# Stick-breaking logits that stay in their PSUM banks, decay products over 128 rows, and the scheduler's price of a matmul column

## The chip, the cores and the metric

The kernel runs on one core of a Trainium2 chip. The metric is the device time of one execution in microseconds (us), taken as the median of the runs; lower is better. Five engines are named as the profile names them: PE (TensorE, its weight loads apart as PEld), DVE (VectorE), ACT (ScalarE), POOL (GpSimd) and SP (SyncE, which issues most DMAs).

## What is computed

The reference is a network of two blocks on 512 tokens of width 1024, all in float32: a short convolution mixer, a gated feed-forward layer, a sparse attention layer ("NSA") and another feed-forward layer; then the second block, which has two mixers side by side, a state-space mixer ("SSD") and a stick-breaking attention of 16 heads, and a third feed-forward layer. The change touches the stick-breaking attention and one product of the SSD mixer:

```python
def stick_breaking_mixer(q, k, v, q_norm_w, k_norm_w):
    ...
        logits = jnp.einsum("bhqd,bhkd->bhqk", qb, kp) * scale
        strict = s_pos[None, :] < t_pos[:, None]
        log_rem = jnp.where(strict, jax.nn.log_sigmoid(-logits), 0.0)
        log_between = lax.cumsum(log_rem, axis=3, reverse=True) - log_rem
        weights = jnp.where(strict, jnp.exp(jax.nn.log_sigmoid(logits) + log_between), 0.0)
        outs.append(jnp.einsum("bhqk,bhkd->bhqd", weights, vp))

def ssd_chunked(x, dt, a, b_mat, c_mat):
    ...
    a_cs = jnp.cumsum(a_dt, axis=-1)
    seg = a_cs[..., :, None] - a_cs[..., None, :]
    decay = jnp.exp(jnp.where(causal, seg, -jnp.inf))
```

For a key s before a query t, the log of the weight is the logit minus the sum of softplus(logit) over the keys from s up to the query.

## The kernel before

**Products.** A float32 product is made of three: each operand is split into a rounded part and a rest (`hilo`, names ending in h and l), and PE multiplies h by h, l by h and h by l, 512 columns at most at a time, into one PSUM bank of 128 x 512. There are eight banks (tag `ps`), and every PSUM tile takes one whole bank from its first product to its last reader. Weights come from HBM in chunks (`raw`), are split by ACT and DVE (`wh`, `wl`) and multiply with the tokens (tiles `d`, and `qk` for the token-major queries, keys and values).

**Stick-breaking.** Each of the 16 heads goes through two generators. `sb_logits` handles the four key tiles of 128 keys in three units: 384 and 128 columns in the first, 256 in the second, 512 in the third. For each unit it multiplies the keys `ks` with the queries `qh` and `ql` into a bank `lg`, and makes the softplus from it: three ACT passes (Abs, Exp, Ln), a DVE pass (`le<-lg,le`), a POOL mask (AFFINE_SELECT), and the split into `ph` and `pl`, which are kept in SBUF. The bank `lg` is free after the DVE pass. `sb_out` comes later: for each unit it takes a new bank `bt`, makes the same logits in it once more (`bt<-qh,ks` and `bt<-ql,ks`), adds the sums of the softplus terms onto them with constant matrices (`ntri`, `nones`, and the mask `rmask` by an identity; all of them are slices of the tile `cr`), and ACT takes the exponential (`we`). The split of that (`w`) is multiplied with the values into `so`. The places in the code:

```python
            todo = [(k, st["qh"][h][:, 128 * kt:512], 0), (k, st["ql"][h][:, 128 * kt:512], 0)]
            todo += [(self.ntri, x[:, o:o + n], 0) for x in ps[u]]
            todo.append((self.ridn, self.rmask, None))
```

**Decay products.** In `ssd_pair`, `weights(h)` spreads one row of the running sums over all partitions with a product `al<-at,er`: the tile `at` has 64 rows (the rounded sums in rows 0 to 15, the rests in rows 32 to 47, zeros between) and `er` picks one of them. There is one such product of 512 columns per head, 16 in all.

**The order.** Nothing runs in the order in which it is written. A `Recorder` notes every instruction; `arrange` then orders them for each engine by a model of its own: `cost` gives each a duration, `forward` lets each engine take what is ready, `backward` gives latest starts, which serve as priorities in the next `forward`. It also chooses the PSUM bank of each tile and, where several engines can do an instruction (`any`), the engine. All helpers issue through one line, so the profile shows L485 for nearly everything: go by tile names. In `weave`, the generators of the second block stand side by side: for each pair of heads the projections, `ssd_pair`, `sb_logits`, `sb_out`, with start and end set by constants (`P0` to `P13`, `SS`, `O0` to `O3`).

Of the kernel before, what the change touches and what calls it, by code (L numbers as in the profile page):

```python
# [11 lines left out]
D = 1024  # L12
# [74 lines left out]
def weave(*streams):  # L87
    """emits instruction streams side by side: (generator, the total of what it yields, start, end)"""
# [21 lines left out]
class View:  # L110
    """an access pattern of a tile that gets its place when the instructions are ordered"""
# [21 lines left out]
class Slot:  # L133
    """one tile as the program sees it, from its first access to its last"""
# [21 lines left out]
class Recorder:  # L156
    """records the instructions of the program, orders those of every engine by the time at which their
    operands are there and by their place in the program, and gives the tiles their places"""
# [8 lines left out]
    # from the end on one engine to the start on another  # L167
# [27 lines left out]
    def any(self, *ways):  # L195
        """one instruction that several engines can do, the usual one first: (engine, method, arguments)"""
# [45 lines left out]
    def cost(self, o, method, a, k, outs, ins):  # L242
        """nanoseconds on the engine, and those of a transfer"""
# [3 lines left out]
        # a scalar per partition  # L247
# [4 lines left out]
        elif o.eng == "tensor":  # L252
            passes = 1 if ins[-1].dtype == F32R else 2 if method == "transpose" else 6
            o.dur = size(outs[0]) * passes / 2.4 + 3.0
            # the next product waits until its own matrix is loaded
            o.load = (int(ins[0].ap.shape[-1]) if method == "matmul" else 128) / 1.2
# [13 lines left out]
    def place(self, ap):  # L270
        """the pattern on the place its tile got"""
# [23 lines left out]
    def backward(self):  # L295
        """the latest starts, from the end of the program"""
# [30 lines left out]
    def forward(self, urgent, look, timed=False):  # L327
# [26 lines left out]
        def avail(t):  # L354
            """when the tile can have a place, or None"""
# [15 lines left out]
        def begin(e, i, limit):  # L371
            """when the engine can start the instruction, or None if not by the limit"""
# [14 lines left out]
            if e in other:  # L387
                # one engine at a time reads a bank
                for t in o.banks:
                    at = max(at, t.read.get(other[e], -1e9) + self.LAG[other[e]][e])  # L390
            if e != o.eng:
                # another engine has to be done with it earlier than the usual one
# [8 lines left out]
        while first < len(ops):  # L401
            best = None
            for e, lst in cand.items():
# [10 lines left out]
                if top is not None and timed and e in self.PATIENT:  # L414
                    # a more urgent one that is ready soon goes first if that makes the later of the two less late
# [74 lines left out]
class Body:  # L490
# [26 lines left out]
    def alike(*views):  # L517
        """whether the Pool engine can do it: in SBUF, on the same partitions, of a size that is worth it"""
# [22 lines left out]
    def copy(self, out, a, scale=None):  # L541
        """a, by a factor"""
# [21 lines left out]
    def load(self, g, parts=None):  # L564
        """starts the transfer of a group of weight blocks"""
# [59 lines left out]
    def dense_g(self, name, n, x, ks=None, m=128):  # L625
        """the same as dense, in steps"""
# [7 lines left out]
    def dense_seq(self, specs, x, ks=None, first=2, late=1):  # L634
        """yields the finished PSUM tile of every (name, n); the late operands are used last in the first tiles,
        or every operand in all of them before the next one"""
# [10 lines left out]
    def dense_halves(self, specs, x, ks=None):  # L647
        """the same for the halves of the tokens, the first halves of all tiles before the second ones"""
# [12 lines left out]
    def dense_late(self, specs, x, first):  # L661
        """dense_seq where the second halves of the tokens come later: the first tiles take them last"""
        out = [self.ps("d") for _ in range(first)]
        for h, sl in enumerate(HALVES):
            for (name, n), p in zip(specs, out):
                # one accumulation group per bank: its first write clears the bank's flags
                self.half(p[:, sl], name, n, x, range(len(x)), sl, h == 0, h == 1)
# [5 lines left out]
    def rsq(self, src, scale, eps):  # L673
        """rsqrt(scale * src + eps) by logarithm and exponential, and a step of Newton"""
# [10 lines left out]
    def allsum(self, acc):  # L685
        """the sums over the partitions, on all of them"""
# [35 lines left out]
    def setup(self):  # L722
# [18 lines left out]
        self.er = self.nc.tile([64, 16], F32R, "er")  # L741
        nc.vector.tensor_copy(self.er, self.cst[0:64, C_E:C_E + 16])
# [965 lines left out]
```

## Time and profile before

| | us |
|---|---|
| median of three timed runs | 2162.2 (2161.71 to 2162.23) |
| the profiled execution, first to last instruction | 2159.8 |
| PE busy in it | 2117.5 |
| DVE busy | 1386.1 |
| ACT busy | 941.8 |
| stretch of the stick-breaking mixer, 1327 to 1759 | 432 |

The profiled execution is told by its span, from the first to the last instruction: 2159.8 us. The timed runs take 2.4 us more, which lie around the span. A row of the timeline has the start, the duration, the engine, and out<-in by tile. Ends of matmuls are modelled, and they overlap: the pace of PE is read from the starts of rows that follow each other.

### The profile page before, as it was taken

The page shows a single profiled execution, that of the slowest core. Times are in us where ns is not written, and L with a number is a line of the kernel's source. Part 1 is how long each engine was busy: PE and PEld are TensorE (multiplying, and loading weights), DVE is VectorE, ACT ScalarE, POOL GpSimd, SP SyncE. Part 2 cuts the span into 40 slices and gives each one's busy share as a digit, 9 for nine tenths or more (in the row PEclk, how much of TensorE's full clock was granted, in tenths as well). Part 3 has the DMA queues.
Part 4 walks back from the last instruction along what each step waited for, and adds up shares of the span by engine and source line. Part 5 has one row for each costly group of instructions (what it writes and reads, how often), then busy time and mean ns, then how long its engine had stood idle before and what let it go on. Part 6 is the DMA issues. An engine that isn't in the chain of part 4 may idle for free.

```text
span 2159.8 us, 28829 instructions
## 1 busy us (share of the span) xinstructions
PE 2117.5 (98%) x11113; PEld 1789.1 (83%) x11113; DVE 1386.1 (64%) x2347; ACT 941.8 (44%) x1587; POOL 425.9 (20%) x558
## 2 busy tenths in 40 slices
PE   8999999999999999999999999999999998999999
PEld 7888888888788777888888887989897888888887
DVE  6578754644868996654355598787879867333333
ACT  4233322332335885322222477677667746222221
POOL 1023320211223763000000141221315222000000
PEclk9999999999999999999999999999999999999999
DMA  4245652533332000222222332111121124222222
GB/s 166 98 178 188 212 183 97 175 117 104 104 127 72 1 1 31 97 98 98 98 98 98 117 127 79 59 50 59 59 69 40 40 95 140 98 98 98 98 98 98
DMA packets 60682, 214.04 MB, mean 99 GB/s; under 512 B 7424, under 2 KB 7552, under 8 KB 60544
## 3 DMA queue, kind: packets, MB, share of 16 engines
q1 hardware_dynamic: 52704, 186.50, 24.9%
q0 software_dynamic: 7840, 25.70, 3.5%
q8 instruction: 87, 1.43, 0.3%
q14 instruction: 51, 0.42, 0.1%
HBM read 210.07 MB, written 2.10 MB: 98 GB/s over the span
## 4 chain that ended last, share of the span: by engine, by line
PE 86%; DVE 9%; ACT 2%; issue 2%; POOL 1%; DMA 0%; SPq 0%; DVEq 0%; ACTq 0%; POOLq 0%
PE d L485 71%; PE qk L485 5%; PE bt L485 2%; PE o L485 2%; DVE wl L485 1%; PE so L485 1%; PE pt L485 1%; PE s L485 1%; DVE pr L485 1%; PE lg L485 1%; DVE e L485 1%; DVE ptl L485 1%; ACT wh L485 1%; DVE ss L485 0%; PE chid L485 0%
## 5 line engine op out<-in xcount | busy, mean ns | idle before, releaser
L485 ACT CAST wh<-raw 128x1024 fp32r<-128x1024 f32 (+1 forms) x332 | 347.6, 1048 | 873.1 <-PE d L485 736.8
L485 DVE TENSOR_TENSOR wl<-raw,wh 128x1024 fp32r<-128x1024 f32 (+1 forms) x342 | 424.6, 1242 | 417.3 <-ACT wh L485 414.5
L485 PE MATMUL d<-xh,wh 128*128 128x512 f32 (+1 forms) x1064 | 417.4, 394 | 6.0 <-ACT xh L485 6.0
L485 PE MATMUL d<-xh,wl 128*128 128x512 f32 (+1 forms) x1064 | 416.5, 392 | 1.0 <-DVE wl L485 1.0
L485 PE MATMUL d<-xl,wh 128*128 128x512 f32 x1064 | 416.3, 391 | 0.0
L485 PE MATMUL d<-hb,wh 128*128 128x512 f32 (+1 forms) x1136 | 332.7, 377 | 3.6 <-ACT hb L485 3.3
L485 PEld LDWEIGHTS d<-xh,wh 128*128 128x128 f32 (+1 forms) x1064 | 200.5, 189 | 47.6 <-ACT xh L485 6.0
L485 PEld LDWEIGHTS d<-hb,wh 128*128 128x128 f32 x1136 | 205.5, 190 | 40.1 <-ACT hb L485 3.5
L485 PEld LDWEIGHTS d<-xh,wl 128*128 128x128 f32 (+1 forms) x1064 | 200.3, 188 | 43.7 <-DVE wl L485 1.8
L485 PEld LDWEIGHTS d<-xl,wh 128*128 128x128 f32 x1064 | 200.4, 188 | 41.6 <-issue 0.7
L485 PE MATMUL d<-hb,wl 128*128 128x512 f32 (+2 forms) x568 | 212.3, 376 | 2.5 <-DVE wl L485 2.5
L485 PE MATMUL d<-hidh,wl 128*128 128x512 f32 (+1 forms) x561 | 211.8, 378 | 0.0
L485 PE MATMUL d<-hidh,wh 128*128 128x512 f32 (+1 forms) x561 | 211.5, 377 | 0.0
L485 PE MATMUL d<-hidl,wh 128*128 128x512 f32 (+1 forms) x561 | 211.5, 377 | 0.0
L485 PE MATMUL qk<-wh,hb 128*128 128x256 f32 x768 | 145.0, 288 | 2.1 <-ACT hb L485 1.0
L485 POOL TENSOR_TENSOR acc<-acc,sq 128x512 f32<-128x512 f32 (+1 forms) x24 | 38.2, 1591 | 499.7 <-ACT sq L485 441.9
L485 PEld LDWEIGHTS qk<-wh,hb 128*128 128x128 f32 x768 | 121.8, 193 | 6.5 <-DVE hb L485 1.5
L485 PEld LDWEIGHTS d<-hb,wl 128*128 128x128 f32 (+1 forms) x568 | 107.3, 190 | 22.6 <-DVE wl L485 3.5
L485 PEld LDWEIGHTS d<-hidl,wh 128*128 128x128 f32 x561 | 105.6, 188 | 19.4
L485 PEld LDWEIGHTS d<-hidh,wh 128*128 128x128 f32 x561 | 105.6, 188 | 19.3
L485 PEld LDWEIGHTS d<-hidh,wl 128*128 128x128 f32 x561 | 105.6, 188 | 19.2
L485 PE MATMUL qk<-wl,hb 128*128 128x256 f32 x384 | 109.0, 286 | 1.5 <-DVE wl L485 1.5
(370 smaller groups left out, 3678.5 us busy)
## 6 DMA issues: line engine op xcount, KB each, us to landing
raw<-in_wall_dram SPq DMA_DIRECT2D x345, 512.0 KB, 3.2
ada<-in_wada_dram POOLq DMA_DIRECT2D x96, 256.0 KB, 4.6
res<-in_x_dram SPq DMA_DIRECT2D x8, 256.0 KB, 7.3
out_dram<-res SPq DMA_DIRECT2D x8, 256.0 KB, 2.0
raw<-in_wall_dram SPq DMA_DIRECT2D x2, 256.0 KB, 3.7
cond<-in_c_dram POOLq DMA_DIRECT2D x2, 256.0 KB, 5.3
cst<-in_consts_dram SPq DMA_DIRECT2D x1, 394.5 KB, 7.0
mst<-in_consts_dram SPq DMA_DIRECT2D x1, 320.0 KB, 3.8
```

Of the source, the lines that this page charges most:

```text
L485: r = getattr(getattr(self.real, o.eng), m)(*[self.place(x) for x in a], **{n: self.place(x) for n, x in k.items()})
```

## The change

Three edits, and no other that does anything (comments and docstrings went too).

First, `sb_logits` leaves its logits in the bank `lg`, with the accumulation open, and hands the bank on with `ph` and `pl`. `sb_out` takes no bank of its own and makes no logits: it adds the sums onto that bank. So a bank is held from the first logits product of a unit to its exponential. Only the first product into the bank has the start flag.

Second, `at` and `er` have 128 rows in place of 64, the added rows zero.

Third, the scheduler's model of a matmul: a column costs 17/16 of a 2.4 GHz cycle (it was one cycle), the fixed part is 1 ns (it was 3), and a weight load is 3 ns dearer. The constants in `weave` are as before.

```diff
+    COLUMN = 17 / 16 / 2.4
...
-            o.dur = size(outs[0]) * passes / 2.4 + 3.0
-            # the next product waits until its own matrix is loaded
-            o.load = (int(ins[0].ap.shape[-1]) if method == "matmul" else 128) / 1.2
+            o.dur = size(outs[0]) * passes * self.COLUMN + 1.0
+
+            o.load = (int(ins[0].ap.shape[-1]) if method == "matmul" else 128) / 1.2 + 3.0
...
-        self.er = self.nc.tile([64, 16], F32R, "er")
-        nc.vector.tensor_copy(self.er, self.cst[0:64, C_E:C_E + 16])
+        self.er = self.nc.tile([128, 16], F32R, "er")
+        nc.vector.tensor_copy(self.er, self.cst[:, C_E:C_E + 16])
...
-        self.at = self.pg(F32R, "at")[0:64]
+        self.at = self.pg(F32R, "at")
...
-            mm(al, self.er[:, hd:hd + 1].to_broadcast([64, 128]), self.at, start=True, stop=True)
+            mm(al, self.er[:, hd:hd + 1].to_broadcast([128, 128]), self.at, start=True, stop=True)
...
+            for i, (kt, o, n) in enumerate(self.UNITS[u]):
+                k = st["k"][h][:, 128 * kt:128 * kt + 128]
+
+                for x in ("qh", "ql"):
+                    self.nc.tensor.matmul(lg[:, o:o + n], k, st[x][h][:, 128 * kt:512], start=i == 0 and x == "qh",
+                                          stop=False, skip_group_check=True)
...
-            ps.append(self.hilo(e, w, name="p"))
+            ps.append(self.hilo(e, w, name="p") + (lg,))
...
-            b = self.ps("bt")
-            # log weight: logit - (sum of the softplus terms from this key to the query)
+            b = ps[u][2]
...
-                todo = [(k, st["qh"][h][:, 128 * kt:512], 0), (k, st["ql"][h][:, 128 * kt:512], 0)]
-                todo += [(self.ntri, x[:, o:o + n], 0) for x in ps[u]]
-                todo.append((self.ridn, self.rmask, None))
+                todo += [(self.ntri, x[:, o:o + n], b[:, o:o + n]) for x in ps[u][:2]]
+                todo.append((self.ridn, self.rmask, b[:, o:o + 128]))
...
+            for j, (mat, x, dst) in enumerate(todo):
+                mm(dst, mat, x, start=False, stop=j == len(todo) - 1, skip_group_check=True)
```

PE has 11099 products before and 10971 with the change; the 128 that are missing are the second logits, 8 per head. The new prices and the missing products reorder all engines. Two places on PE are shown here, with the numbers of the tiles.

The sums of the 512-column unit of the first head, before: a bank of their own, which starts with the two logits products.

```order
L485 MATMUL bt_11715<-qh_11195,ks_11298 128x512
L485 MATMUL bt_11715<-ql_10600,ks_11298 128x512
L485 MATMUL bt_11715<-ph_11622,cr_73 128x512
L485 MATMUL bt_11715<-pl_11637,cr_73 128x512
L485 MATMUL bt_11715<-cr_73 128x128
L485 MATMUL bt_11715<-ph_11444,cr_73 128x384
L485 MATMUL bt_11715<-pl_11467,cr_73 128x384
```

The same sums with the change, in the bank that the logits were left in; the products of the SSD mixer (`y`) follow after the third.

```order
L486 MATMUL lg_11537<-ph_11597,cr_73 128x512
L486 MATMUL lg_11537<-pl_11607,cr_73 128x512
L486 MATMUL lg_11537<-cr_73 128x128
L486 MATMUL y_11649<-mh_11554,xdh_11412 64x128
L486 MATMUL y_11649<-ml_11564,xdh_11412 64x128
```

The two logits products are gone, and the rest of the sums stands further on.

The second place is in the middle of the mixer, where the first half of the output projection (`d<-ysh`, `share` in the code) starts: the 256-column logits of a head and what follows them. Before:

```order
L485 MATMUL lg_13718<-qh_13029,ks_13024 128x256
L485 MATMUL lg_13718<-ql_13048,ks_13024 128x256
L485 MATMUL d_13724<-ysh_13689,wh_13414 128x512
L485 MATMUL d_13726<-ysh_13689,wh_13641 128x512
L485 MATMUL d_13724<-ysl_13710,wh_13414 128x512
L485 MATMUL d_13724<-ysh_13689,wl_13443 128x512
L485 MATMUL d_13724<-ysh_13694,wh_13414 128x512
```

With the change, where `ph_13684` and `pl_13689` are the two parts of the softplus of these very logits:

```order
L486 MATMUL lg_13664<-qh_12963,ks_12974 128x256
L486 MATMUL lg_13664<-ql_12959,ks_12974 128x256
L486 MATMUL lg_13561<-ph_13684,cr_73 128x256
L486 MATMUL lg_13664<-ph_13684,cr_73 128x256
L486 MATMUL d_13696<-ysh_13687,wh_13358 128x512
L486 MATMUL lg_13561<-pl_13689,cr_73 128x256
L486 MATMUL lg_13561<-ph_13612,cr_73 128x128
L486 MATMUL lg_13561<-pl_13618,cr_73 128x128
```

Before, the products of the projection follow the logits; with the change the sums over these logits' own softplus stand right behind them, with no product between. At two more places of the new order few products stand between a unit's logits and the first product with its `ph`: 14 (a 256-column unit) and 16 (the 512-column unit after it). The next smallest are 23 and 33; in the order before, no unit has fewer than 50 there.

## Rows read from the trace of the kernel before

**Rows 1.** The page, its first lines: span, busy time of the engines.
```profile
span 2159.8 us, 28829 instructions
PE 2117.5 (98%) x11113; PEld 1789.1 (83%) x11113; DVE 1386.1 (64%) x2347; ACT 941.8 (44%) x1587; POOL 425.9 (20%) x558
```

**Rows 2.** Windows: start:end, length, busy by engine, granted clock, DMA share, GB/s.
```profile
567.00:842.00 275.00, 263.91 (x1614) 215.89 (x1613) 236.82 (x659) 178.78 (x482) 126.80 (x189) 0.99 0.15 52
...
1327.00:1759.00 432.00, 423.79 (x2854) 378.35 (x2854) 348.21 (x577) 300.75 (x517) 120.28 (x155) 1.00 0.16 56
```

**Rows 3.** Waits of PE, 1327 to 1759: us in total, times, longest.
```profile
PE bt L485 <- DVE ks L485: 2.1, 1, 2.1
PE so L485 <- DVE w L485: 1.5, 3, 0.7
```

**Rows 4.** Timeline of PE, 1370 to 1378.
```profile
1370.28 0.40 PE L485 MATMUL lg<-ql,ks 128*128 128x512 f32 x1
1370.51 0.33 PE L485 MATMUL bt<-qh,ks 128*128 128x384 f32 x1
1370.69 0.34 PE L485 MATMUL bt<-ql,ks 128*128 128x384 f32 x1
...
1371.73 0.27 PE L485 MATMUL bt<-qh,ks 128*128 128x128 f32 x1
1371.84 0.28 PE L485 MATMUL bt<-ql,ks 128*128 128x128 f32 x1
...
1377.16 0.28 PE L485 MATMUL bt<-ql,ks 128*128 128x256 f32 x1
1377.28 0.28 PE L485 MATMUL bt<-ph,cr 128*128 128x256 f32 x1
```

**Rows 5.** Instructions of tile bt: ns min/median/max, first and last start, forms.
```profile
L485 PE MATMUL bt<-qh,ks x64: 220/333/501, 1352.1 to 1751.6; 128*128 128x512 f32 x16, 128*128 128x384 f32 x16, 128*128 128x128 f32 x16, 128*128 128x256 f32 x16
```

**Rows 6.** Instructions of tile al.
```profile
L485 PE MATMUL al<-at,er x16: 491/497/498, 1334.9 to 1697.1; 64*128 64x512 f32 x16
```

**Rows 7.** Timeline of PE around the first al.
```profile
1334.91 0.50 PE L485 MATMUL al<-at,er 64*128 64x512 f32 x1
1335.34 0.33 PE L485 MATMUL st<-xsh,btokh 128*128 128x128 f32 x1
```

**Rows 8.** Timeline of all engines, 1370 to 1377: the softplus of one 512-column unit.
```profile
1370.74 0.59 ACT L485 ACTIVATE le<-lg 128x512 f32<-128x512 f32 x1
...
1372.65 1.29 ACT L485 ACTIVATE le<-le 128x512 f32<-128x512 f32 x2
1373.97 0.69 DVE L485 SCALAR_TENSOR_TENSOR le<-lg,le 128x512 f32<-128x512 f32 x1 [2.19 <-ACT le L485]
1374.79 0.29 POOL L485 TENSOR_SCALAR_AFFINE_SELECT le<-le 128x128 f32<-128x128 f32 x1 [15.34 <-DVE le L485]
1375.29 0.61 ACT L485 CAST ph<-le 128x512 fp32r<-128x512 f32 x1
1376.09 0.68 DVE L485 TENSOR_TENSOR pl<-le,ph 128x512 fp32r<-128x512 f32 x1
```

**Rows 9.** Groups by form, 1327 to 1759: count | busy us, mean ns | idle before.
```profile
L485 ACT ACTIVATE le<-le 128x256 f32<-128x256 f32 x32 | 13.3, 417 | 0.6
L485 DVE SCALAR_TENSOR_TENSOR le<-lg,le 128x256 f32<-128x256 f32 x16 | 6.7, 417 | 2.9 <-ACT le L485 2.8
L485 ACT ACTIVATE le<-lg 128x256 f32<-128x256 f32 x16 | 6.1, 381 | 3.8 <-PE lg L485 3.7
L485 ACT CAST ph<-le 128x256 fp32r<-128x256 f32 x10 | 4.1, 407 | 6.8 <-POOL le L485 6.6
```

**Rows 10.** Timeline of PE around 1652.
```profile
1650.77 0.40 PE L485 MATMUL so<-w,svl 128*64 128x512 f32 x1
1653.26 0.50 PE L485 MATMUL bt<-qh,ks 128*128 128x512 f32 x1 [2.09 <-DVE ks L485]
```

**Rows 11.** A window of 10 us from 1655 (columns as in rows 2).
```profile
1655.00:1665.00 10.00, 8.08 (x51) 6.85 (x50) 8.53 (x12) 5.83 (x13) 5.02 (x7) 0.83 0.01 2
```

More of the change, by code (lines that the diff above doesn't have):

```diff
@@ L1531, with sb_logits @@
     UNITS = (((1, 0, 384), (3, 384, 128)), ((2, 0, 256),), ((0, 0, 512),))
-    def sb_lg(self, hd, out, u, stop):
+    def sb_logits(self, hd):
+        ps = []
         st = self.st[hd // 2]
         h = hd % 2
-        for kt, o, n in self.UNITS[u]:
-            k = st["k"][h][:, 128 * kt:128 * kt + 128]
-            self.nc.tensor.matmul(out[:, o:o + n], k, st["qh"][h][:, 128 * kt:512], start=True, stop=False)
-            self.nc.tensor.matmul(out[:, o:o + n], k, st["ql"][h][:, 128 * kt:512], start=False, stop=stop)
-    def sb_logits(self, hd):
-        ps = []
         for u in range(3):
@@ L1546, in sb_logits @@
             lg = self.ps("lg")
-            self.sb_lg(hd, lg, u, True)
+            for i, (kt, o, n) in enumerate(self.UNITS[u]):
[3 more added lines that the diff above has]
+                                          stop=False, skip_group_check=True)
             e = self.pg(name="le")[:, 0:w]
@@ L1561, in sb_out @@
         ps = self.pp.pop(hd)
-        st = self.st[hd // 2]
         h = hd % 2
@@ L1573, in sb_out @@
             w = sum(n for _, _, n in self.UNITS[u])
-            b = self.ps("bt")
+            b = ps[u][2]
+            todo = []
             for kt, o, n in self.UNITS[u]:
-                k = st["k"][h][:, 128 * kt:128 * kt + 128]
-                todo = [(k, st["qh"][h][:, 128 * kt:512], 0), (k, st["ql"][h][:, 128 * kt:512], 0)]
-                todo += [(self.ntri, x[:, o:o + n], 0) for x in ps[u]]
-                todo.append((self.ridn, self.rmask, None))
+                todo += [(self.ntri, x[:, o:o + n], b[:, o:o + n]) for x in ps[u][:2]]
+                todo.append((self.ridn, self.rmask, b[:, o:o + 128]))
                 for k2 in range(kt + 1, 4):
@@ L1583, in sb_out @@
                     n2 = 512 - 128 * k2
-                    todo += [(self.nones, x[:, o2:o2 + n2], n - n2) for x in ps[u2]]
-                for j, (mat, x, c) in enumerate(todo):
-                    dst = b[:, o:o + 128] if c is None else b[:, o + c:o + n]
-                    mm(dst, mat, x, start=j == 0, stop=j == len(todo) - 1)
+                    todo += [(self.nones, x[:, o2:o2 + n2], b[:, o + n - n2:o + n]) for x in ps[u2][:2]]
+            for j, (mat, x, dst) in enumerate(todo):
+                mm(dst, mat, x, start=False, stop=j == len(todo) - 1, skip_group_check=True)
             e = self.pg(name="we")[:, 0:w]
```

## Prediction

> **What bounds the kernel now.** I read the page first: PE is busy for 2117.5 of 2159.8 us, 98%, and no other engine passes 64% [rows 1]. An average can hide a stage with another limit, so next come the windows. In the stick-breaking stretch, 1327 to 1759, PE is busy for 423.8 of 432 us, DVE for 348.2, ACT for 300.8 [rows 2]; the reader is to see that PE sets the pace there too, with 8.2 us idle, and that DVE at 81% has room, though not much. In the sparse attention, 567 to 842, PE is idle for 275 - 263.9 = 11.1 us [rows 2]. The waits say what ends the idle time of the stretch: single waits for DVE, the largest 2.1 us once for `ks` and 1.5 us in three for `w` [rows 3]. So a product that goes is worth its pace on PE as long as the products behind it find their operands ready. That condition is what the rest turns on.
>
> The pace is read from starts, since ends of matmuls are modelled. A 512-column product is followed after 1370.51 - 1370.28 = 0.23 us, one of 384 after 0.18, one of 256 after 0.12; one of 128 columns is followed after 0.11 where the next needs a new matrix [rows 4].
>
> **The change, part by part.**
>
> *Removed logits.* Per head the second logits go: two products each of 512, 384, 256 and 128 columns, 64 with `qh` [rows 5] and as many with `ql`. By the pace that is 2 x (0.23 + 0.18 + 0.12 + 0.11) = 1.28 us per head, 20.5 us in 16 heads. All of it lies on PE, in the stretch where PE is 98% busy. A lower bound: if the 128-column products behind the gap now wait for their own matrices, each of the 32 small ones gives back no more than half of 0.11, and 20.5 - 32 x 0.055 = 18.7 remains. I take 20.3, near the upper end, since the big products carry most of it.
>
> *Padded decay products.* An `al` has 512 columns like the product of 0.23 us, but the next product starts 1335.34 - 1334.91 = 0.43 us after it [rows 7], and there are 16 [rows 6]. The one visible difference is its 64 rows. With 128 rows I price it as the other 512-column products: -0.2 x 16 = -3.2 us. If the cause is the operand that is spread by a stride of zero, which stays, it is 0; those are the bounds. I take -3.2: every other 512-column product with 128 rows, whatever its operands, shows 0.23. Against this stands a rule of the Trainium skill ("TensorE: Matmul & The Clock Gate", section "Why this matters for your kernels"): a single product over 32 rows takes the same time as one over 128, and fewer rows pay only by letting several run at once. By it the padding would give nothing, and the sum would be 3.2 us higher; the row with 0.43 speaks against it for 64 rows.
>
> *Chains that were covered.* Between a unit's logits and the first product with its softplus lie three ACT passes, a DVE pass, a POOL mask and a cast. For a 512-column unit the trace shows 1370.28 to 1375.90, 5.6 us, of which 1.3 is ACT doing other work (1371.33 to 1372.65) [rows 4, 8]; so 4.3 us at least. For 256 columns the durations are 0.38 + 2 x 0.42 + 0.42 + 0.29 + 0.41 = 2.3 us [rows 8, 9], and with hand-offs as in the 512-column case, about 1.2 us in all, 3.5. Before, at least 50 products stood in between. In the new order one unit has none, and PE, which takes its products in order, has to sit out about 3.5 us there, and 0.4 more for `pl` (0.68 behind `ph` [rows 8], one product of 0.23 between). Two more units have 14 and 16 products, worth 2.4 and 2.6 us at the pace above, where 3.5 and 4.3 are wanted: 1.1 and 1.7. Together 6.7, call it 7. Behind PE wait all products that follow, and through them ACT and DVE, so nothing else hides it. The bounds: 4 if only the first shows, 12 if ACT is in between with other work, as in the row.
>
> *The clock.* After a gap of 1653.26 - 1650.77 = 2.5 us [rows 10] the next window shows a granted clock of 0.83 over 10 us [rows 11]: 3.4 us at 1.2 in place of 2.4 GHz, worth 1.7 us of PE's work. A 3.5 us gap should do the same: +1.7 (0 to 3.4).
>
> *Banks.* Before, `lg` was free after the DVE pass, 1374.66 - 1370.28, some 4.4 us after its last logits product [rows 4, 8]; now it is held until the exponential, and where sums come late, for tens of us. Eight banks serve everything, so `qk`, `d`, `so`, `y` and `al` find fewer. No row shows a wait for a bank that is short. The bounds are nothing and a second 8.2 us, the whole idle time of the stretch [rows 2] once more; I take 2, near the lower end: the order is made with the banks in view, and would be late mainly where its own model errs.
>
> *The new prices.* They remove no work, they only move it. The old model priced a 512-column product at 216 ns, the new one at 228; the rows say 0.23. An order that is made with the true pace should bring operands less often late: of the 8.2 us idle in the stretch I take 2 as gone (of the 3.6 in [rows 3]), with bounds 0 and 8.2. The sparse attention is reordered too; its 11.1 idle us [rows 2] could shrink or grow by half, ±5, and I take 0. What idles elsewhere, 42.3 - 11.1 - 8.2 = 23 us, I leave as it is.
>
> The sum against the profiled execution: 2159.8 - 20.3 - 3.2 + 7 + 1.7 + 2 - 2 = 2145.0. The timed runs lie 2.4 us above their span, so 2147.4, or 2147 against 2162.2: 15 us, 0.7%.
>
> **The rivals.** *All of it arrives.* The three near places are covered, because what precedes them runs late anyway, and the better prices take 2 us of waits: 2162.2 - 23.5 - 2 = 2136.7. For it speaks that ACT and DVE have room; against it the unit with no product behind its logits.
>
> *The padding gives nothing.* `al` stays at 0.43 us: 2150.6. For it, that no 64-row product with other operands is there to compare; against it, that 0.43 is close to twice 0.23. (The rule of the Trainium skill above would make it so.)
>
> *Given back.* The chains take their upper end, 12, each of the three gaps costs the clock 1.7, and the banks 8: 2162.2 - 23.5 + 12 + 5.1 + 8 - 2 = 2161.8, no change. For it: between 1655 and 1665 DVE is busy for 8.53 of 10 us and PE for only 8.08 [rows 11], so there are places where PE already isn't the bound and fewer products give nothing.
>
> *Slower: the banks run dry.* Mechanism: a head in `sb_out` holds three banks, the next head's units up to three more, a pair of `qk` two; then a new `lg` or `d` waits until an exponential is done. The place is every unit, 48 of them. It decides from 23.5 / 48 = 0.49 us per unit; one exponential, 0.59 like the Abs of a bank [rows 8], with its hand-off of 0.2 on each side is about 1 us, and were that uncovered in two thirds of the units, 32 us: 2162.2 - 23.5 + 32 = 2170.7. For it: the banks are held longer by a factor of several. Against it: the order is made with the banks in view, and only three near places were found. The Trainium skill has a rule on this side ("PSUM — Partial Sum Buffer", "Summary: rules for kernel authors"): "Evacuate promptly". No row here prices its breach.
>
> **Chances.** My forecast, 2141 to 2154, 0.62; all arrives, 0.14; padding gives nothing, 0.06; given back, 0.10; slower, 0.08. A measurement of this kernel can tell about 0.2%, 4.3 us, from no change. Of the case given back, a fifth is still faster by that and the rest the same: faster 0.84, same 0.08, slower 0.08. The range for 8 in 10 takes the likeliest whole, most of the case in which all arrives, and the faster part of the one given back: 2136 to 2158.
>
> **What would show it.** In the changed profile: no `bt`; PE products fewer by 128; starts 0.23 us apart behind `al`; the stretch of the mixer 15 us shorter at like DVE time; a new wait of PE for `ph` of 3 to 5 us once in the middle of the mixer, and a granted clock below 1 behind it; two of 1 to 2 us near the last third. Wrong would be: waits of `qk` or `d` for ACT's `we` in many places (the banks), a sparse attention that is longer by more than 5 us, or `al` still at 0.43.

## The result and the profile after

The changed kernel takes 2189.5 us (2186.54 to 2192.65, four runs), the kernel before beside it 2161.95. The ratio is 1.0129, 95% interval 1.0115 to 1.0144. That is 27.6 us slower, where 15 us faster was forecast; the range ended at 2158.

The page of the changed kernel, span and engines:

```profile
span 2189.1 us, 28533 instructions
PE 2117.0 (97%) x10985; PEld 1780.6 (81%) x10985; DVE 1420.1 (65%) x2351; ACT 941.8 (43%) x1577; POOL 437.9 (20%) x564
```

PE has 128 products fewer than in [rows 1] and yet is busy for as long: 2117.0 against 2117.5 us. The products that are left ran more slowly, so the first thing to ask is where the clock was low. Windows answer that. I cut the program at marks that every kernel here has: the attention from its first `chid` to its last `o`, and the mixers from the first `qk` to the last `so`, as the tiles' views give them. A window is read from the one profiled execution, whose time can differ from the median (by 3.3 us at most here, f1_late_b2). First the mixers before the change (columns as in rows 2: start:end, length, busy by engine, granted clock, DMA share, GB/s).

```profile
1248.00:1759.00 511.00, 496.93 (x3271) 439.97 (x3272) 420.89 (x685) 356.19 (x612) 147.38 (x189) 0.99 0.19 64
```

The same two stretches of the changed kernel, the attention first:

```profile
569.00:851.00 282.00, 265.76 (x1602) 214.93 (x1601) 242.14 (x669) 178.16 (x475) 125.42 (x183) 0.99 0.15 51
1262.00:1789.00 527.00, 492.53 (x3138) 431.90 (x3138) 429.86 (x674) 351.69 (x598) 165.08 (x199) 0.96 0.18 62
```

The mixers, where all the removed work lay, take 527 us in place of 511. PE is idle there for 34.5 us in place of 14.1, so 20 us are new waits. Its busy time fell by 4.4 us only, where the prediction had removed 23.5, so 19 us came back in it. Most of that is the clock. Eight stretches of the changed kernel's mixers were granted 0.50, which is 1.2 GHz, where there were two before. The sums of the windows over these stretches, after and then before:

```profile
sum 45.40, PE 39.80 PEld 33.58 DVE 37.24 ACT 30.23 POOL 16.63; mean PE 4.98 PEld 4.20 DVE 4.65 ACT 3.78 POOL 2.08
sum 10.20, PE 8.63 PEld 7.18 DVE 10.17 ACT 8.91 POOL 4.67; mean PE 4.32 PEld 3.59 DVE 5.08 ACT 4.45 POOL 2.33
```

PE worked for 31 us more at half the clock, which is 16 of the 19 us; the other 3 aren't traced. The attention, which the change of the code doesn't touch, is 8 us longer (282 against 274, in rows 2 cut at 275), and 6 us more lie before and between the two stretches: the attention starts at 569 in place of 567, the mixers 411 us after its end in place of 407.

The waits of PE in the mixers after the change (us in total, times, longest), the largest ones:

```profile
PE lg L486 <- ACT ph L486: 5.4, 2, 4.9
PE d L486 <- ACT ysh L486: 2.8, 1, 2.8
PE d L486 <- ACT qh L486: 2.7, 1, 2.7
PE tq L486 <- ACT ysb L486: 2.5, 1, 2.5
PE y L486 <- DVE ysb L486: 2.1, 1, 2.1
PE y L486 <- DVE e L486: 1.9, 1, 1.9
...
PE lg L486 <- ACT we L486: 1.0, 2, 0.7
```

Before, the longest single wait was 2.1 us [rows 3]. Two kinds stand here. `lg` waits for `ph` and `d` for `ysh` because they multiply them. But `d` has no product with `qh`, and `tq` none with `ysb`. What such a wait is for shows in the timeline of the changed kernel, all engines, at those two places:

```profile
1428.14 0.39 PE L486 MATMUL lg<-ql,ks 128*128 128x512 f32 x1
1430.51 0.68 ACT L486 ACTIVATE qh<-tq,vecs 64x512 fp32r<-64x512 f32 x1
1431.24 0.80 PE L486 MATMUL d<-hb,wh 128*128 128x512 f32 x1 [2.71 <-ACT qh L486]
...
1460.67 1.21 POOL L486 TENSOR_SCALAR_AFFINE_SELECT le<-le 128x128 f32<-128x128 f32 x1 [5.20 <-DVE le L486]
1461.91 0.62 ACT L486 CAST ph<-le 128x512 fp32r<-128x512 f32 x1 [3.39 <-POOL le L486]
1462.44 0.57 ACT L486 COPY ysb<-so 64x512 f32<-64x512 f32 x1
1463.06 0.33 PE L486 MATMUL tq<-cst,qn 128*128 128x128 f32 x1 [2.52 <-ACT ysb L486]
```

`d<-hb,wh` starts 0.05 us after ACT has read the last of a `tq` (1430.51 + 0.68), and `tq<-cst,qn` 0.05 us after ACT has copied a `so` out (1462.44 + 0.57). `tq` and `so` are PSUM tiles: so these products wait for the reader of a bank that they are to take. In the second place the reader was late because ACT, in its own order, first stood 3.39 us for a POOL mask that belongs to the softplus. Waits for `we`, which I had named as the sign of this, are small (1.0 us in two for `lg`): a product seldom waits for the long-held bank itself, but for whichever of the remaining ones the order gave it.

All waits of PE in a mixer window can be sorted in this way, by the instruction that the profile names as the last to release the product. Waits for an instruction that makes none of the product's operands but reads a PSUM tile, so for a bank, come to 18.7 us in 18 waits in the changed kernel and to 0.3 us in one before; waits for operands come to 13.9 and 14.4 us. So nearly all of the 20 us of new idle time are waits for banks, and the new waits for operands, `ph` among them, took the place of others.

### The profile page after: what moved, and what is told of

Its sections match the earlier page's. It is cut to its first block, busy times and chain, and to the rows that moved or that the text cites. A ratio compares the mean times of both kernels' runs of the same rounds, so it can differ in the third digit from the quotient of the medians.

```text
span 2189.1 us, 28533 instructions
## 1 busy us (share of the span) xinstructions
PE 2117.0 (97%) x10985; PEld 1780.6 (81%) x10985; DVE 1420.1 (65%) x2351; ACT 941.8 (43%) x1577; POOL 437.9 (20%) x564
## 4 chain that ended last, share of the span: by engine, by line
PE 79%; DVE 12%; ACT 4%; issue 2%; POOL 2%; DMA 0%; SPq 0%; DVEq 0%; POOLq 0%; ACTq 0%
PE d L486 68%; PE qk L486 3%; PE o L486 2%; DVE wl L486 2%; PE lg L486 1%; DVE pr L486 1%; PE s L486 1%; PE so L486 1%; POOL res L486 1%; PE pt L486 1%; ACT le L486 1%; DVE ptl L486 1%; ACT wh L486 1%; DVE e L486 1%; PE y L486 0%
## 5 line engine op out<-in xcount | busy, mean ns | idle before, releaser
L486 DVE TENSOR_TENSOR wl<-raw,wh 128x1024 fp32r<-128x1024 f32 (+1 forms) x341 | 448.5, 1316 | 420.5 <-ACT wh L486 419.6
L486 PE MATMUL d<-xh,wh 128*128 128x512 f32 x1064 | 416.5, 392 | 6.7 <-ACT xh L486 6.7
L486 PE MATMUL d<-hb,wh 128*128 128x512 f32 (+2 forms) x1136 | 334.9, 379 | 10.2 <-ACT hb L486 4.0
L486 PEld LDWEIGHTS d<-hb,wh 128*128 128x128 f32 (+1 forms) x1136 | 206.5, 191 | 48.2 <-ACT hb L486 4.2
L486 PEld LDWEIGHTS d<-xh,wh 128*128 128x128 f32 x1064 | 200.3, 188 | 48.5 <-ACT xh L486 6.7
L486 POOL TENSOR_TENSOR acc<-acc,sq 128x512 f32<-128x512 f32 (+1 forms) x21 | 32.7, 1556 | 483.4 <-ACT sq L486 461.4
```

The source lines that it names most:

```text
L486: r = getattr(getattr(self.real, o.eng), m)(*[self.place(x) for x in a], **{n: self.place(x) for n, x in k.items()})
```

## The experiments

The table collects the windows of all runs, cut at the same marks (the attention of the expectations, 190 us before and 196.5 in e1_price, begins later, at the first `s`); idle is the length less PE's busy time. The time is the median, the ratio is to the kernel before, run on the same chip.

| run | us | ratio, 95% interval | attention | mixers | PE idle in them | clock in them |
|---|---|---|---|---|---|---|
| before | 2162 | | 274 | 511 | 14.1 | 0.99 |
| the change | 2189.5 | 1.0115 to 1.0144 | 282 | 527 | 34.5 | 0.96 |
| e1_price | 2178.1 | 1.0059 to 1.0092 | 283 | 514 | 15.2 | 0.99 |
| e2_logits | 2166.3 | 1.0013 to 1.0032 | 274 | 514 | 24.1 | 0.97 |
| e3_rows | 2156.3 | 0.9964 to 0.9985 | 274 | 505 | 14.6 | 0.99 |
| e4_drop | 2146.3 | 0.9914 to 0.9944 | 274 | 497 | 16.3 | 0.98 |
| e7_six | 2195.2 | 1.0133 to 1.0174 | 286 | 527 | 35.2 | 0.96 |
| e8_part | 2157.0 | 0.9968 to 0.9987 | 274 | 507 | 18.4 | 0.98 |
| e9_rl | 2163.5 | 1.0001 to 1.0023 | 274 | 513 | 26.6 | 0.97 |
| e11_late | 2153.4 | 0.9949 to 0.9981 | 273 | 501 | 20.9 | 0.98 |
| e5_cheap | 2177.9 | 1.0053 to 1.0093 | 279 | 516 | 17.6 | 0.99 |
| e6_slack | 2169.5 | 1.0021 to 1.0048 | 279 | 512 | 16.6 | 0.99 |
| e10_col101 | 2162.1 | 0.9993 to 1.0016 | 276 | 509 | 10.8 | 0.99 |
| e12_margin | 2163.7 | 0.9998 to 1.0020 | 273 | 510 | 13.1 | 0.99 |
| f4_col103 | 2167.2 | 1.0015 to 1.0034 | 279 | 511 | 12.4 | 0.99 |
| f3_dve6 | 2174.1 | 1.0041 to 1.0071 | 276 | 513 | 14.5 | 0.99 |
| f2_rl_b2 | 2175.0 | 1.0046 to 1.0076 | 272 | 525 | 37.9 | 0.97 |
| f1_late_b2 | 2166.9 | 1.0012 to 1.0030 | 273 | 513 | 26.7 | 0.98 |

**The edits one by one.** The first four runs split the change.

e1_price: the third edit alone.

```diff
-            o.dur = size(outs[0]) * passes / 2.4 + 3.0
+            o.dur = size(outs[0]) * passes * self.COLUMN + 1.0
...
```

> The kernel before with the third edit alone (a matmul column priced at 17/16 of a cycle, weight loads 3 ns dearer). If the new price is what costs (theory A: it takes away slack that the too cheap price had left between PE and the engines that feed it), the sparse attention gets about 10 us longer and the mixer too: 2175 to 2195 us. If the held banks are what costs (theory B), the price alone does little: 2157 to 2167 us.

It cost 16.4 us by itself, and little of it in the mixers. The two windows of e1_price, the attention first:

```profile
569.00:852.00 283.00, 266.46 (x1608) 215.58 (x1606) 242.60 (x669) 178.15 (x475) 125.14 (x184) 0.99 0.16 51
1262.00:1776.00 514.00, 498.79 (x3268) 440.39 (x3269) 422.57 (x688) 359.30 (x613) 134.06 (x173) 0.99 0.19 63
```

The attention is 9 us longer, the mixers 3; the rest lies before and between them. The attention of the whole change, 282 us, is this one. PE is idle in it for 16.5 us in place of 11.1, in waits that each grew by little: `chid` for `wl` 4.2 us where it was 3.4 before, `pt` for `pr` 2.1 where it was 0.8, `pct` for `pc` 1.7 where it was 0.4.

e2_logits: the first edit alone, with the old price (its part of the diff above).

> The kernel before with the first edit alone (logits stay in their banks, no second logits, old price, 64-row decay products). Theory A: the removed products count, 2141 to 2152 us, attention as before. Theory B: the banks cost more than the products give, 2170 to 2192 us, with the loss in the mixer.

e4_drop: the same products go, but each unit still takes a second bank for its sums, and the first is free after the DVE pass. It leaves the logits out of the weights, so it is a probe and not a kernel to use.

```diff
-                todo = [(k, st["qh"][h][:, 128 * kt:512], 0), (k, st["ql"][h][:, 128 * kt:512], 0)]
-                todo += [(self.ntri, x[:, o:o + n], 0) for x in ps[u]]
+                todo = [(self.ntri, x[:, o:o + n], 0) for x in ps[u]]
```

> The kernel before without the second logits in the banks bt: the logits are left out of the weights, all else is as before, and no bank is held longer. It is the removal without the banks. Theories A and B: about 20 us less, 2138 to 2147 us. Theory C (PE isn't what bounds the mixer, so its products are worth nothing): 2155 us or more.

The pair is the centre of the study: both make the same products, and differ in how long the logits' bank is held (and in the sums being chained to it). e2_logits took 2166.3 us and e4_drop 2146.3: keeping the logits in their banks costs 20 us, more than the 15.4 that the missing products save. The time of e2_logits lies between its two forecasts. The mixers of e2_logits:

```profile
1249.00:1763.00 514.00, 489.90 (x3139) 427.10 (x3140) 431.89 (x681) 355.74 (x605) 165.26 (x198) 0.97 0.19 63
```

The mixers of e4_drop:

```profile
1249.00:1746.00 497.00, 480.66 (x3143) 424.37 (x3144) 425.23 (x687) 355.86 (x612) 141.37 (x184) 0.98 0.20 66
```

The profiled executions lie 16.5 us apart (2165.3 and 2148.8 us), which is what the windows show. Of their 17 us, 7.8 are more idle time of PE (24.1 against 16.3) and 9.2 are more busy time at a like number of products (3139 and 3143). The clock explains about 5 of the 9.2: PE worked at 0.50 for 27.2 us against 16.7. The rest isn't traced. Waits for a bank come to 9.5 us in e2_logits and 3.1 in e4_drop, waits for operands to 15.3 and 14.7. The longest for a bank, two of e2_logits and one of e4_drop:

```profile
PE d L485 <- DVE ks L485: 3.1, 2, 2.7
PE qk L485 <- ACT we L485: 2.0, 1, 2.0
...
PE st L485 <- DVE xp L485: 0.8, 1, 0.8
```

`d` doesn't multiply `ks`, nor `qk` `we`, nor `st` `xp`. So most of the idle time that keeping the logits adds is waiting for banks, and not for the chain from logits to sums.

e3_rows: the second edit alone.

```diff
-        self.at = self.pg(F32R, "at")[0:64]
+        self.at = self.pg(F32R, "at")
...
```

> The kernel before with the second edit alone (decay products over 128 rows). Both theories: al is followed after 0.23 us in place of 0.43, 16 times, so about 2159 us, if the order stays much the same; if rows don't matter to a product, al stays at 0.43 and the time at 2162 us.

It gained 5.4 us, where the pace behind `al` alone gives 3.2. PE has the same order in both traces, so the same place can be compared, before and then in e3_rows:

```profile
1476.19 0.28 PE L485 MATMUL qk<-wl,hb 128*128 128x256 f32 x1
1476.40 0.50 PE L485 MATMUL al<-at,er 64*128 64x512 f32 x1
1476.83 0.50 PE L485 MATMUL qk<-wh,hb 128*128 128x256 f32 x2
1477.17 0.28 PE L485 MATMUL qk<-wl,hb 128*128 128x256 f32 x1
...
1475.49 0.28 PE L485 MATMUL qk<-wl,hb 128*128 128x256 f32 x1
1475.61 0.40 PE L485 MATMUL al<-at,er 128*128 128x512 f32 x1
1475.84 0.40 PE L485 MATMUL qk<-wh,hb 128*128 128x256 f32 x2
1476.08 0.28 PE L485 MATMUL qk<-wl,hb 128*128 128x256 f32 x1
```

The next product starts 0.23 us after `al`, where it was 0.43 with 64 rows, as forecast. But the neighbours gain too: `al` starts 0.12 us after the product in front of it in place of 0.21, and the two products behind it take 0.24 us in place of 0.34. Together that is 0.39 us (0.98 against 0.59), in 16 places 6.2 us, and it covers the 5.4.

**Is it the banks?** e2_logits could also be slow by the chain from logits to sums. Three runs change how many banks there are, or for how long they are held.

e7_six: e4_drop, which holds no logits (and leaves them out of the weights), with six banks.

```diff
-        return self.nc.tile([128, 512], F32, name, "ps", 8, True)
+        return self.nc.tile([128, 512], F32, name, "ps", 6, True)
```

> The kernel without the second logits (as in e4_drop, the logits are left out of the weights) on six PSUM banks in place of eight. The held banks of the first edit are worth nearly two banks on average. If scarcity of banks is what costs in the mixer (theory B), the stretch from the first to the last so, 361 us in e4_drop, becomes 372 to 390 us, and short waits for readers of a bank appear in front of d, qk, y, tq. If the chains between logits and sums are what costs (theory B2), no sums get nearer to their logits here and the stretch stays within 5 us of 361.

2195.2 us, 49 more than e4_drop. The mixers, without any near chain between logits and sums:

```profile
1266.00:1793.00 527.00, 491.81 (x3143) 430.66 (x3142) 430.57 (x684) 350.09 (x598) 154.59 (x195) 0.96 0.19 62
```

The stretch from the first to the last `so` is 386 us, inside the forecast for scarce banks. The mixers' 527 us, 35.2 idle and clock 0.96 are close to the change's 527, 34.5 and 0.96, but the change has the new price too; the like comparison is e2_logits (514, 24.1, 0.97). Waits for a bank come to 14.5 us, for operands to 20.4. Among its waits are products that wait for a tile that they don't multiply, `st` for `le` and `d` for `we`:

```profile
PE st L485 <- DVE le L485: 4.0, 1, 4.0
...
PE d L485 <- ACT we L485: 2.4, 2, 1.3
```

Two banks fewer cost the other stages too (attention 286), so only the mixers' 30 us (527 - 497) compare with the kept logits' 17 (514 - 497). Taking banks away is thus enough to cost this much; how many banks the kept logits are worth isn't measured.

e8_part: the second edit, and the logits kept for the 512-column unit alone, a third of the banks.

```diff
+    KEEP = (2,)
...
-            ps.append(self.hilo(e, w, name="p"))
+            ps.append(self.hilo(e, w, name="p") + ((lg,) if u in self.KEEP else ()))
...
```

> Padded decay products, old price, and logits that stay in their bank for the 512-column unit alone, which is made last and summed first; the other units make them anew. It gives back 16 x 2 x 0.23 = 7.4 us of products and holds a third of the banks, for the shortest time. Theory B: most of it arrives, 2148 to 2153 us. If the near chain of logits and sums is what costs (theory B2): this unit is the one whose sums come soonest, so 2153 to 2162 us.

2157.0 us, as e3_rows without any kept logits (2156.3): with a third of the banks held, the cost eats the 7.4 us that the removed products bring. That time was forecast for theory B2, the near chain, but the waits say banks: `lg` waits 0.3 us for `ph` in all, while waits for a bank come to 7.7 us, against 1.1 in e3_rows.

e9_rl: the first two edits with the old price. It is the base of the next one.

> The first two edits together, at the old price. If the edits add up: 4.5 for the logits and -5.4 for the rows, 2160 to 2162 us, and the 28 us that the whole change loses over the kernel before are then the price's, in the attention and again in the mixer. If the banks cost more where PE is faster: 2166 us or more.

2163.5 us, 1.9 above before, where the two alone add up to +4.6 - 5.4 = -0.8. This too lies between the forecasts.

e11_late: e9_rl with the logits of a head made later, and so held for less long. The streams of `sb_logits` run from 0.35 to 0.55 of a head pair's step behind their old start, in place of from 0 to 0.38.

```diff
-                st += [(self.sb_logits(2 * i + h), 3, o, o + P9), (self.sb_out(2 * i + h), 6, o + P10, o + P11)]
+                st += [(self.sb_logits(2 * i + h), 3, o + 0.35, o + 0.55), (self.sb_out(2 * i + h), 6, o + P10, o + P11)]
```

> The first two edits at the old price, with the logits of each head written 0.35 to 0.55 into its pair in place of 0 to 0.38, the sums as before. Fewer banks stay open in the new order (2.0 for logits on average in place of 2.6, by PE's work in the order). Theory B: the mixer gets 4 to 12 us shorter than with the first two edits alone. If it is not the time for which banks are held: no shorter.

2153.4 us: 10 us less than e9_rl, at the same products. It is the fastest here that computes everything. The mixers:

```profile
1248.00:1749.00 501.00, 480.08 (x3139) 424.61 (x3139) 427.91 (x696) 345.79 (x602) 137.00 (x182) 0.98 0.20 65
```

Waits for a bank fell from 12.5 us in e9_rl to 1.9, waits for operands rose from 15.7 to 18.9, and the largest is now the near chain, six times over:

```profile
PE lg L485 <- ACT ph L485: 5.6, 6, 2.1
```

So the chain and the banks pull against each other: logits made early hold banks, logits made late let PE wait for the softplus. At these places the chain is the cheaper of the two. e4_drop with late logits wasn't run, so what the later start would be worth with no bank held isn't known.

**Why does the price cost?** e1_price made no product more or less, and its column is nearer to the rows' 0.23 us than the old one. Two explanations: the old, cheap column gave useful slack, or the constants in `weave` fit the old price, and any other one costs.

e5_cheap: a column of 15/16 cycle, as far off on the other side.

```diff
+    COLUMN = 15 / 16 / 2.4
...
-            o.dur = size(outs[0]) * passes / 2.4 + 3.0
+            o.dur = size(outs[0]) * passes * self.COLUMN + 3.0
```

> The kernel before with a matmul column priced at 15/16 of a cycle, so cheaper still than before (fixed part and weight load as before): the other direction. If a cheap price leaves slack between PE and the engines that feed it (theory A1), attention takes its 190 us or less and the time is 2157 to 2164 us. If any price other than the one that the constants were found with costs (theory A2), attention gets longer here too: 2167 us or more.

2177.9 us, as slow as the dear one, as theory A2 has it: the reason isn't slack alone. Its attention is longer by 5 us, its mixers by 5.

e6_slack: the new price, with 200 ns more in the model for every hand-off to PE.

```diff
-        "vector": {"tensor": 202.0, "vector": 127.0, "scalar": 128.0, "gpsimd": 155.0, "sync": 100.0},
+        "vector": {"tensor": 402.0, "vector": 127.0, "scalar": 128.0, "gpsimd": 155.0, "sync": 100.0},
...
-        "scalar": {"tensor": 216.0, "vector": 131.0, "scalar": 143.0, "gpsimd": 155.0, "sync": 100.0},
+        "scalar": {"tensor": 416.0, "vector": 131.0, "scalar": 143.0, "gpsimd": 155.0, "sync": 100.0},
...
-        "gpsimd": {"tensor": 135.0, "vector": 120.0, "scalar": 85.0, "gpsimd": 100.0, "sync": 100.0},
+        "gpsimd": {"tensor": 335.0, "vector": 120.0, "scalar": 85.0, "gpsimd": 100.0, "sync": 100.0},
```

> The kernel before with the new price of the third edit, and 200 ns more in the scheduler's model for every hand-off from VectorE, ScalarE and GpSimd to TensorE: the true price with slack of another kind. Theory A1: attention comes back from 196.5 to 187 to 192 us, and the total to 2155 to 2167 us. Theory A2: it stays at 2172 us or more.

2169.5 us, half of the 16 us back, and the attention, as the expectation measures it, 193.0 us: between the two theories. With e5_cheap this shows no more than that another pair of numbers gives another order, a better one here.

e10_col101 and e12_margin move a number by little: a column of 1.01 cycle, and a constant that sets how much sooner an `any` instruction must be done on another engine.

```diff
+    COLUMN = 1.01 / 2.4
...
-    MARGIN = 704.3
+    MARGIN = 720.0
```

> The kernel before with a column priced at 1.01 cycles, a change of one part in a hundred. If what costs is any order other than the one that the constants were found with (theory A2), this small change costs nearly as much as the large ones, 2166 to 2178 us, most of it before the mixer. If the cost grows with the distance of the price (theory A3), it is 2161 to 2164 us.

> The kernel before with the scheduler's constant MARGIN at 720.0 in place of 704.3, which decides only when another engine may take over an instruction, and has nothing to do with a matmul's price. Theory A2 (any other order costs): 2164 to 2178 us. If the price of a matmul is special: 2161 to 2163 us.

2162.1 and 2163.7 us, 0.5 and 2.1 more than the kernel before beside them, neither clear of noise. e12_margin says little: by the tile names in the traces, 10979 of PE's 11113 products keep their old order among themselves. In e10_col101 10601 do, and in e1_price 10376. f4_col103 goes half way to the change's price, and f3_dve6 moves VectorE's price by the same 1/16 instead.

```diff
+    COLUMN = 1.03 / 2.4
...
-            o.dur = n * (6.26 if method == "reciprocal" else 0.52 if fast else 1.042) + 68 + (61 if one else 0)
+            o.dur = n * (6.26 if method == "reciprocal" else 0.52 if fast else 1.107) + 72 + (61 if one else 0)
```

> The kernel before with a column at 1.03 cycle in the model, half way to the change's 17/16 (1.01 cost nothing, 17/16 with its other parts 16 us). If the cost grows with the distance from the price that the constants were found with: 2166 to 2172. If it sets in at once past a small distance: 2175 to 2180. If it is chance from order to order: anything from 2158 to 2180.

> The kernel before with another price moved by about the same share: VectorE's instructions 17/16 dearer in the model (1.107 ns for 1.042 per element, 72 for 68 fixed), matmuls as before. If any price that is some 6% off the one that the constants were found with costs as the matmul's did: 2170 to 2180. If only a wrong pace of PE costs, since PE is the bound: 2162 plus or minus 4.

2167.2 us half way and 2174.1 with the other engine's price. So on the dear side the cost grows with the distance from the old price: 0.5 us at 1%, 5 at 3%, 16 at 6% (with the other parts of the third edit). One point on the cheap side costs 16 at 6%, and DVE's price 12 at 6%. How far the order moves doesn't set the cost: f4_col103 moves about as many products out of the old order as e1_price (715 and 737) and costs 5 us where that costs 16. But each price was tried in one order only, so the runs show that other prices cost, and not why. Nor is it one sore place: e1_price lost most in the attention, f3_dve6 little in either stretch (2 us each) and 5 between them, 844 to 1256 in place of 841 to 1248. The two windows of f3_dve6:

```profile
568.00:844.00 276.00, 266.56 (x1608) 215.52 (x1607) 237.94 (x657) 179.06 (x481) 126.03 (x189) 0.99 0.15 51
1256.00:1769.00 513.00, 498.52 (x3264) 438.22 (x3265) 416.97 (x665) 356.62 (x609) 159.22 (x196) 0.99 0.19 62
```

**More than the sum.** The edits alone come to +16.4 + 4.6 - 5.4 = 15.6 us; together they cost 27.6. Two runs use the new price from the second block's mixers on only: f2_rl_b2 on top of e9_rl, f1_late_b2 on top of e11_late.

```diff
+    PRICE = (1 / 2.4, 3.0, 0.0)
...
-            o.dur = size(outs[0]) * passes / 2.4 + 3.0
+            o.dur = size(outs[0]) * passes * self.PRICE[0] + self.PRICE[1]
...
+        nc.PRICE = (17 / 16 / 2.4, 1.0, 3.0)
         drain(self.sb_qk2(hb))
```

> Edits 1 and 2 as in the change, the new price from the second block's mixers on only. It splits the 26 us by which the whole change is longer than edits 1 and 2 with the old price (2189.5 against 2163.5). If the loss lies before the mixers (attention 196.5 for 190, the gated layer 410 for 407), 26 minus about 15 goes: 2175, with a mixer like the changed kernel's (387 us between the first and the last so). If the mixer under the new price is as good as under the old, 2163 to 2165. If all of the 26 is the mixer's, 2187 or more.

> Edits 1 and 2 with the logits streams later (as in the run with 2153.4 us), and the new price from the second block's mixers on; the code before them is priced as before. Theory A (the price costs because the constants were found with the old one, wherever it is used): the mixer's constants were also found with it, so the mixer gives back about as much as the attention did, 6 to 15 us, 2160 to 2168. Theory B (the price only costs before the mixer, where the single-edit run lost it): 2153 plus or minus 3, with 366 us between the first and the last so. Theory C (price and long-held banks together cost, because the dearer columns make the sums later against the logits): with the banks held for less, a part of the 10 us that the whole change lost beyond the sum of its edits, 2154 to 2160.

f2_rl_b2 took 2175.0 us. That splits the 26 us between e9_rl and the whole change: 11.5 come from the price in the mixers, 14.5 from the price before them. That is the first of its three forecasts. f1_late_b2 took 2166.9, 13.5 more than e11_late, inside the forecast of theory A. So the price costs the mixers 12 to 14 us once the logits are kept, with the banks held long or less long, and 3 without (514 against 511 in e1_price). So the long hold isn't what makes the price dearer. The waits of f2_rl_b2 say where the time goes:

```profile
PE lg L486 <- ACT ph L486: 9.7, 3, 6.1
PE lg L486 <- ACT we L486: 4.8, 3, 2.2
```

These two come to 14.5 us, where e9_rl with the old price has 3.1 and 0.4; that is as much as 11.0 of the 11.3 us by which PE is idle for longer (37.9 against 26.6). The sums stand closer behind their softplus in this order, and new logits closer behind the exponentials. f1_late_b2 doesn't repeat it: its `lg` waits 3.6 us for `ph`, less than the 5.6 of e11_late, and its longer mixers have no one place in the waits.

## Why the prediction was wrong, point by point

- **What bounds it.** Right, and the condition named with it, that a removed product is worth its pace "as long as the products behind it find their operands ready", is where it broke. It should have read: operands and a free bank. (The last step of the sum is off by 0.7 us: a run lasts 1.7 us longer than its own span, 2190.83 against 2189.1, and not 2.4.)
- **Removed logits, -20.3.** The price by pace stands; e4_drop, where they go and nothing is held, gained 15.4. The idle time and the clock behind new waits took the other 5 (idle 14.1 to 16.3 us; PE at 0.50 for 16.7 us in place of 8.6, worth 4).
- **Padding, -3.2.** Right in the mechanism and too small: 5.4 in all, since the neighbours of `al` were slow too and the working looked only behind it. The next product starts 0.23 us after `al` in place of 0.43, so the rival in which padding gives nothing falls. The Trainium skill's rule for few rows ("TensorE: Matmul & The Clock Gate", "Why this matters for your kernels") speaks of 32 rows; for 64 rows the measurement here decides against carrying it over.
- **Near chains, +7.** The first place showed, longer than the 3.9 us that were worked out for it, the other two hardly (0.5 us for `ph` in all). PE in the changed kernel:

```profile
1536.98 0.28 PE L486 MATMUL lg<-ql,ks 128*128 128x256 f32 x1
1542.13 0.79 PE L486 MATMUL lg<-ph,cr 128*128 128x256 f32 x2 [4.87 <-ACT ph L486]
...
1547.49 0.63 PE L486 MATMUL d<-ysh,wh 128*128 128x512 f32 x1
1547.92 0.63 PE L486 MATMUL d<-ysl,wh 128*128 128x512 f32 x1
...
1550.21 0.40 PE L486 MATMUL d<-ysl,wh 128*128 128x512 f32 x1
1550.45 0.39 PE L486 MATMUL d<-ysh,wl 128*128 128x512 f32 x1
```

  A gap of 5.15 us from start to start. The sum of 7 was about right, but these waits took the place of others: waits for operands didn't grow in all (13.9 us against 14.4).
- **The clock, +1.7: mis-sized.** Behind that gap 512-column products start 0.43 us apart (1547.49, 1547.92) and only later 0.24 (1550.21, 1550.45). The granted clock by stretches of 5 us from 1537 on:

```profile
1537.00:1542.00 5.00, 0.26 (x2) 0.05 (x1) 4.81 (x6) 2.49 (x8) 2.95 (x3) 0.76 0.00 0
1542.00:1547.00 5.00, 4.83 (x16) 4.08 (x17) 5.00 (x6) 4.10 (x8) 4.64 (x6) 0.50 0.00 0
1547.00:1552.00 5.00, 5.00 (x17) 3.98 (x16) 4.64 (x7) 2.99 (x4) 0.33 (x1) 0.71 0.04 7
1552.00:1557.00 5.00, 5.00 (x23) 4.14 (x23) 2.44 (x3) 1.05 (x1) 0.00 (x0) 1.00 0.27 101
```

  After the gap, 5 x 0.50 + 5 x 0.29, about 4 us of PE's work, is lost at 1.2 GHz in place of 2.4, so the 5 us gap cost 9. And the term stood for one gap where there were many: over the mixers 16 us went this way, beside 20 us of new waits.
- **Banks, +2 with bounds 0 to 8.2: the step that failed.** Held banks cost 20 us (e2_logits against e4_drop, chains and clock within it), and waits for banks went from 0.3 us before to 18.7 in the changed kernel. "The order is made with the banks in view" was no ground for the lower end: what it has in view is its own model, and on the chip PE waited for readers of banks that came late, as at 1462 in the changed kernel. The upper bound was no bound either; I had taken the idle time once more, with nothing that ties one to the other. The slower rival had the better price, 1 us in two thirds of 48 units, 32 us; measured are 20, which is 0.42 per unit, a little short of the 0.49 from which it decides. That the price is near is in part luck: the waits for banks are not one in two thirds of the units, but 11 in e2_logits and 18 in the changed kernel, some of them long. So the first two edits alone come out about even. The Trainium skill's "Evacuate promptly" ("PSUM — Partial Sum Buffer", "Summary: rules for kernel authors") agrees with the runs, which now give it a price here.
- **New prices, -2, and ±5 in the attention: the other step that failed.** They cost 16.4 us alone, and 26.0 on top of the first two edits (2189.5 against 2163.5). I had reasoned that a truer pace makes a better order, with no row behind it; the sign of being wrong that was named, an attention longer by more than 5 us, came true with 8. A likely reason is that the other constants of the order (`P0` to `P13` and the like) go with the less true price; a price off on either side costs (e1_price, e5_cheap), but that reason itself isn't shown.
- **The rivals.** The first two edits without the third come out as "given back" (2163.5 against 2161.8 worked out). With the third, the slower side came true, with its mechanism in place but not alone: 20 us for banks and chains, 16 for the price, 12 for the edits at once, less 15.4 and 5.4, are the 27.6.

What stays open: why the price costs the mixers 12 us once the logits are kept and 3 otherwise is shown only for the long hold, as far as the waits go (`lg` for `ph` and `we`), and not for the short one; and finding the constants anew, for the new price or for the kept logits, wasn't tried, so how much of either cost would then go isn't known.

## What to carry to other kernels

A result that stays in PSUM saves the products that would make it again, and costs a bank for the whole time between; before pricing it, count banks and time held, and make it as late as the chain behind it allows (e11_late: 10 us back). Where the clock falls behind a wait of PE, the wait costs more than the gap: 5 us became 9 at one place, 20 became 36 over the changed mixers. A scheduler's constants can fit one set of prices, true or not; here the three prices that were moved by 6%, one of them nearer to the trace, and the one moved by 3% made the order worse while the constants stayed.

## What the runs showed of the hardware that wasn't expected

A 512-column product over 64 rows that stands between products over 128 rows costs 0.39 us more than the same one padded to 128, at a granted clock of 1.00: 0.20 behind itself, 0.09 in front of it, 0.10 behind the next product. All 16 stand alone like this, so what several in a row would cost isn't shown. And the cost of idle time through the clock can come near to the idle time: 16 us beside 20 in the changed kernel, 5 beside 7.8 between e2_logits and e4_drop.
